# The high and low parts of the activations start where the weights' tiles do, modulo 512 bytes

## The chip, the cores and the metric

The kernel runs on one core of one Trainium2 chip. Its time is the device time of one execution in microseconds (us). Three executions of the kernel before took 716.81, 717.13 and 719.08 us; the median is 717.13 us. The instruments are a hardware profile of one execution (its page and its trace, which can be asked for groups of instructions, waits, the chain of work that ended last, and the instructions in order of time) and, for addresses, the built program.

## The reference, cut to what matters

A two-layer encoder trunk over 512 tokens of width 1024, in float32. The first layer is a Mamba-2 mixer, the second a differential attention:

```python
x = mamba2_layer(x, ...)        # rms_norm, h @ w_in (1024 x 6176), conv, SiLU, chunked scan, gate, @ w_out (2048 x 1024)
kv = rms_norm(x, kv_norm_g) @ w_kv                  # 1024 x 2048, shared keys and values
qg = rms_norm(x, norm_g) @ w_in                     # 1024 x 2048, queries and gate
weights = probs[:, :, 0] - lam * probs[:, :, 1]     # two softmax maps per head, 8 heads
x = x + (out * silu(gate)) @ w_out                  # 1024 x 1024
return rms_norm(x, final_norm_g)
```

Nearly all the arithmetic is in the five large products with a weight matrix. The rest (scan, scores, softmax) is small beside them.

## The kernel before, in words

**Split products.** Each large product runs on TensorE in the type fp32r. To keep float32 accuracy, both factors are split into a high part (rounded to fp32r) and a low part (what is left), and `mm3` (line 243) issues three matmuls: high by high, high by low, low by high. A weight segment arrives by DMA in a tile `raw`; ScalarE writes its high part `whi` (times a gain), VectorE the low part `wlo` (`load`, lines 125 to 179). Two buffers of each rotate. The activations have their own pairs of tiles:

- `hh, hl` (tiles `a_hi`, `a_lo` for the first layer; `b_hi`, `b_lo` for the second, in the same place): the normalised input, 8 blocks of 128 features by 512 tokens (`new_h`, line 342);
- `yh, yl`: the mixer's gated output, per group of 256 features (line 653); the input `xt` shares the buffers of `yl`;
- `oh, ol`: the attention's gated output, per head (line 884).

**What a matmul reads.** TensorE holds one operand of 128 columns in its array (a weight load, LDWEIGHTS, reads it) and streams the other one, 512 columns mostly, past it. While one matmul streams, the load for the next one runs. Both read SBUF. Which tile is loaded and which is streamed differs by product:

| product | PSUM tile | loaded | streamed, columns | matmuls |
|---|---|---|---|---|
| x, B, C of layer 1 | `pg` | `whi`/`wlo` | `a_hi`/`a_lo`, 512 | 768 |
| z of layer 1 | `pz` | `a_hi`/`a_lo` | `whi`/`wlo`, 512 | 384 |
| out projection, layer 1 | `po` | `yh`/`yl` | `whi`/`wlo`, 512 | 384 |
| keys, queries, gate | `pk`, `pq`, `pt` | `whi`/`wlo` | `b_hi`/`b_lo`, 512 | 576 |
| values | `pv` | `b_hi`/`b_lo` | `whi`/`wlo`, 256 | 384 |
| out projection, layer 2 | `pb`, `pc` | `oh`/`ol` | `whi`/`wlo`, 512 | 192 |

The names `po` and `pt` are also used for small float32 matmuls: attention values and states of the scan (`po`), transposed weights of the attention (`pt`). The segment of the out projection that comes last in layer 1 (`("o", 3, 1)`) keeps its split weights in the two buffers of `dec` instead (line 136), 48 of the `po` matmuls.

**Order.** A timeline scheduler of the framework orders the first layer; a dense stream of the large products (`stream_a`) is mixed there with the scan's small matmuls (`ssd`). The second layer's order is written out (`ORDER_B`, `beside`), with the attention of one head beside the dense stream.

**Addresses.** Pools of tiles lie one behind the other in a partition: `const`, `res`, `wp` (`raw`, `whi`, `wlo`), `small`, then the pools of the stage, among them `bp2` (`yl`, `zs`, `xc`, `yh`). A tile starts at a multiple of 32 bytes. `scales` (line 312) takes its tile `r_col`, 16 bytes in a place of 32, from `res`. Every slice that TensorE reads of the tiles above starts a multiple of 512 bytes (128 columns) into its tile, so that all slices of a tile have the tile's own address modulo 512.

Of the kernel before, what the change touches and what calls it, by code (L numbers as in the profile page):

```python
# [9 lines left out]
F32 = mybir.dt.float32  # L10
# [7 lines left out]
P = 128  # L18
S = 512
D = 1024  # L20
NT = S // P
# [42 lines left out]
def trunk(ctx, tc, x, x_t, par, w_dt, w_in, w_out, w_kvqg, w_bo, d_skip, lam_qk, fin_g, out):  # L64
# [4 lines left out]
    const = ctx.enter_context(tc.tile_pool(name="const", bufs=1))  # L69
    res = ctx.enter_context(tc.tile_pool(name="res", bufs=1))  # L70
# [15 lines left out]
    def long_bank(name):  # L86
        return psum.tile([P, 512], F32, tag="long", name=name)
# [163 lines left out]
    def rsqrt(v, n, tag, bufs=2):  # L251


        y = small.tile([P, n], F32, tag=f"{tag}_y", name=f"{tag}_y", bufs=bufs)
        c = small.tile([P, n], F32, tag=f"{tag}_c", name=f"{tag}_c", bufs=bufs)
        iy = small.tile([P, n], I32, tag=f"{tag}_i", name=f"{tag}_i", bufs=bufs)

        def vyy():
            if n == 1:
                V.scalar_tensor_tensor(out=c, in0=y, scalar=v, in1=y, op0=ALU.mult, op1=ALU.mult)  # L260
            else:
                V.tensor_tensor(out=c, in0=y, in1=v, op=ALU.mult)
                V.tensor_tensor(out=c, in0=c, in1=y, op=ALU.mult)

        V.tensor_scalar(out=iy, in0=v.bitcast(I32), scalar1=1, scalar2=None, op0=ALU.logical_shift_right)
        V.tensor_scalar(out=y.bitcast(I32), in0=iy, scalar1=-1.0, scalar2=float(0x5F3759DF - 2 ** 31), op0=ALU.mult, op1=ALU.add)
        vyy()
        V.scalar_tensor_tensor(out=c, in0=c, scalar=-10.0 / 3.0, in1=c, op0=ALU.add, op1=ALU.mult)
        V.scalar_tensor_tensor(out=y, in0=c, scalar=5.0, in1=y, op0=ALU.add, op1=ALU.mult)
        vyy()  # L270
        root_end[0] = V.scalar_tensor_tensor(out=y, in0=c, scalar=-64.0 / 3.0, in1=y, op0=ALU.add, op1=ALU.mult)
        return y
# [39 lines left out]
    def scales(tag, ss):  # L312

        V.tensor_scalar(out=ss, in0=ss, scalar1=ROOT2 / D, scalar2=ROOT2 * EPS, op0=ALU.mult, op1=ALU.add)
        col = res.tile([P, NT], F32, tag="r_col", name=f"{tag}r_col")
        V.tensor_copy(col, rsqrt(ss, NT, "y"))
        w = small.tile([P, NT + 1, P], F32, tag="wide", name=f"{tag}diag", bufs=2)
        GP.memset(w[:, NT], 1.0)
        for t in range(NT):
            GP.tensor_tensor(out=w[:, t], in0=ident, in1=col[:, t:t + 1].to_broadcast([P, P]), op=ALU.mult)  # L320
        ps = long_bank(f"{tag}ps_r")
        T.on = True
        T.matmul(ps, lhsT=w[:, NT], rhs=w[:, 0:NT].rearrange("p t n -> p (t n)"), start=True, stop=True)
        T.on = False
        row = res.tile([P, S], F32, tag="r_row", name=f"{tag}r_row")
        A.copy(row, ps)
        return col, row
# [28 lines left out]
    bctx = ExitStack()  # L356
    bp = bctx.enter_context(tc.tile_pool(name="bp", bufs=1))
    bp2 = bctx.enter_context(tc.tile_pool(name="bp2", bufs=2))

    zt = {}  # L360
    yT = {}
# [42 lines left out]
    for t in range(NT):  # L404
        squares(ss, t)
    r_col, r_row = scales("a", ss)
    V.tensor_scalar(out=sg1, in0=prm[:, C_SG:C_SG + 1], scalar1=0.5 * (1.0 - LAM0), scalar2=None, op0=ALU.mult)
    dtw_raw = sm.tile([P, KD, H], F32, name="dtw_raw")
# [548 lines left out]
    def half(t, n):  # L957
        hs = slice(n * 512, (n + 1) * 512)
        return x_tok[:, t, hs], fg[:, hs], ot[t][:, hs], out[t * P:(t + 1) * P, hs]
# [123 lines left out]
    y, f, o, dst = half(3, 0)  # L1083
# [8 lines left out]
    y, f, o, dst = half(3, 1)  # L1092
# [68 lines left out]
```

## Time and profile before

| | |
|---|---|
| median of three executions | 717.13 us (716.81 to 719.08) |
| the profiled execution: span from its first to its last instruction | 715.2 us |
| TensorE matmuls | 706.5 us busy, 4030 instructions |
| TensorE weight loads | 590.5 us busy |
| VectorE, ScalarE, GpSimd | 521.3, 430.4, 113.5 us busy |
| granted TensorE clock, mean | 0.998 |

How to read it: the matmuls' ends are modelled, and each overlaps the next, so busy TensorE is not TensorE at its peak. What a matmul costs in a stream is its step, the time from its start to the start of the next. The chain of waits lists pieces such as "PE pg L55 x79" with a start and a length: the length over the count is the mean step in that piece. Line 55 is the wrapper through which all instructions of TensorE, VectorE and ScalarE go, so groups are told apart by tiles.

### The profile page before, as it was taken

The page shows a single profiled execution, that of the slowest core. Times are in us where ns is not written, and L with a number is a line of the kernel's source. Part 1 is how long each engine was busy: PE and PEld are TensorE (multiplying, and loading weights), DVE is VectorE, ACT ScalarE, POOL GpSimd, SP SyncE. Part 2 cuts the span into 40 slices and gives each one's busy share as a digit, 9 for nine tenths or more (in the row PEclk, how much of TensorE's full clock was granted, in tenths as well). Part 3 has the DMA queues.
Part 4 walks back from the last instruction along what each step waited for, and adds up shares of the span by engine and source line. Part 5 has one row for each costly group of instructions (what it writes and reads, how often), then busy time and mean ns, then how long its engine had stood idle before and what let it go on. Part 6 is the DMA issues. An engine that isn't in the chain of part 4 may idle for free.

```text
span 715.2 us, 10916 instructions
## 1 busy us (share of the span) xinstructions
PE 706.5 (99%) x4030; PEld 590.5 (83%) x4030; DVE 521.3 (73%) x1197; ACT 430.4 (60%) x955; POOL 113.5 (16%) x158
## 2 busy tenths in 40 slices
PE   9999999999999999999999999999999999999996
PEld 7787888888888888888888879888988898889885
DVE  5579964889579569558996857557667857785886
ACT  6839672664744636537535357667667766765556
POOL 0108411403306025041110101000000000000002
PEclk9999999999999999999999999999999999999999
DMA  8643323233133331331122310421311131122003
GB/s 297 246 177 122 119 62 122 111 119 118 60 118 118 116 120 61 113 123 60 60 81 98 118 59 12 156 77 62 115 60 60 60 119 59 60 80 98 30 0 118
DMA packets 13493, 70.88 MB, mean 99 GB/s; under 512 B 1792, under 2 KB 3328, under 8 KB 6016
## 3 DMA queue, kind: packets, MB, share of 16 engines
q1 hardware_dynamic: 13008, 69.90, 27.3%
q8 instruction: 32, 0.52, 0.3%
q10 hardware_dynamic: 432, 0.28, 0.1%
q14 instruction: 21, 0.17, 0.1%
HBM read 68.02 MB, written 2.16 MB: 98 GB/s over the span
## 4 chain that ended last, share of the span: by engine, by line
PE 90%; ACT 4%; DMA 3%; DVE 2%; issue 1%; SPq 0%; ACTq 0%; DVEq 0%
PE pg L55 21%; PE po L55 17%; PE pz L55 9%; PE pt L55 8%; PE pv L55 6%; PE pq L55 6%; PE pk L55 6%; PE pb L55 3%; PE pc L55 3%; DMA raw<-in_w_in 3%; PE sc L55 3%; PE pyd L55 2%; ACT whi L55 1%; PE pxt L55 1%; PE psA L55 1%; PE pyt L55 1%
## 5 line engine op out<-in xcount | busy, mean ns | idle before, releaser
L55 DVE SCALAR_TENSOR_TENSOR wlo<-raw,prm,whi 128x512 fp32r<-128x512 f32 (+1 forms) x256 | 151.6, 640 | 56.6 <-ACT whi L55 56.2
L55 ACT ACTIVATE whi<-raw,prm 128x512 fp32r<-128x512 f32 (+1 forms) x256 | 136.8, 606 | 65.5 <-issue 13.5
L55 PE MATMUL pg<-a_hi,whi 128*128 128x512 f32 x256 | 103.4, 404 | 0.0
L55 PE MATMUL pg<-a_lo,whi 128*128 128x512 f32 x256 | 102.5, 400 | 0.0
L55 PE MATMUL pg<-a_hi,wlo 128*128 128x512 f32 x256 | 101.3, 401 | 0.0
L55 DVE SCALAR_TENSOR_TENSOR xc<-pg,prc,xc 128x511 f32<-128x511 f32 (+2 forms) x96 | 69.9, 740 | 7.5 <-ACT xc L55 7.1
L55 PEld LDWEIGHTS pg<-a_hi,whi 128*128 128x128 f32 x256 | 48.1, 188 | 11.1 <-issue 0.2
L55 PEld LDWEIGHTS pg<-a_hi,wlo 128*128 128x128 f32 x256 | 48.1, 188 | 11.1
L55 PEld LDWEIGHTS pg<-a_lo,whi 128*128 128x128 f32 x256 | 48.1, 188 | 10.9
L55 PE MATMUL po<-whi,yh 128*128 128x512 f32 x128 | 51.2, 400 | 0.4 <-ACT yh L55 0.4
L55 PE MATMUL po<-wlo,yh 128*128 128x512 f32 x128 | 51.3, 401 | 0.0
L55 PE MATMUL po<-whi,yl 128*128 128x512 f32 x128 | 50.6, 399 | 0.0
L55 PE MATMUL pz<-wlo,a_hi 128*128 128x512 f32 x128 | 50.1, 400 | 0.0
L55 PE MATMUL pz<-whi,a_hi 128*128 128x512 f32 x128 | 49.9, 404 | 0.0
L55 PE MATMUL pz<-whi,a_lo 128*128 128x512 f32 x128 | 49.4, 395 | 0.0
L966 POOL TENSOR_TENSOR ot<-x_tok,fg 128x512 f32<-128x512 f32 x4 | 5.0, 1287 | 248.0 <-DVE x_tok L55 248.0
L55 ACT ACTIVATE s<-s,mx 128x128 f32<-128x128 f32 (+3 forms) x64 | 35.5, 556 | 9.6 <-DVE mx L55 9.1
L593 POOL TENSOR_TENSOR xe<-xdt,tok 128x256 f32<-128x256 f32 x24 | 14.0, 613 | 164.9 <-DVE xdt L55 164.9
L55 ACT ACTIVATE xc<-pg,prc 128x512 f32<-128x512 f32 x32 | 24.8, 775 | 25.0 <-DVE pg L55 19.8
L55 DVE CUSTOM_DVE_ANT_0 s<-sc,bias 128x128 f32<-128x128 f32 (+3 forms) x64 | 29.4, 488 | 12.1 <-PE sc L55 11.7
L55 PE MATMUL pv<-whi,b_hi 128*128 128x256 f32 x128 | 36.6, 286 | 0.0
L55 PE MATMUL pv<-wlo,b_hi 128*128 128x256 f32 x128 | 35.7, 279 | 0.0
(238 smaller groups left out, 1680.5 us busy)
## 6 DMA issues: line engine op xcount, KB each, us to landing
raw<-in_w_in SPq DMA_DIRECT2D x22, 1024.0 KB, 4.8
raw<-in_w_kvqg SPq DMA_DIRECT2D x16, 1024.0 KB, 4.8
dec<-acs_d SPq DMA_DIRECT2D x8, 1024.0 KB, 4.9
raw<-in_w_out SPq DMA_DIRECT2D x8, 1024.0 KB, 4.7
raw<-in_w_bo SPq DMA_DIRECT2D x4, 1024.0 KB, 4.7
x_tok<-in_x SPq DMA_DIRECT2D x4, 512.0 KB, 9.1
out<-ot SPq DMA_DIRECT2D x6, 256.0 KB, 2.4
raw<-in_w_in SPq DMA_DIRECT2D x4, 256.0 KB, 4.5
```

The source lines that it names most:

```text
L55: i = op(*args, **kw)
L593: GP.tensor_tensor(out=xe[:, c], in0=xdt[:, c], in1=toe_tok[:, c, hs].unsqueeze(2).to_broadcast([P, R, HD]), op=ALU.mult)
L966: GP.tensor_tensor(out=o, in0=y, in1=f, op=ALU.mult)
```

## The change

`r_col` is taken from the pool `const` instead of `res`, and the pool `bp2` begins with a tile of 384 bytes that nothing uses:

```diff
     def scales(tag, ss):
...
-        col = res.tile([P, NT], F32, tag="r_col", name=f"{tag}r_col")
+        col = const.tile([P, NT], F32, tag="r_col", name=f"{tag}r_col")
...
     bp2 = bctx.enter_context(tc.tile_pool(name="bp2", bufs=2))
+
+    bp2.tile([P, 96], F32, name="shift", bufs=1)
```

The first edit moves the tiles between the old and the new place of `r_col` up by 32 bytes, the second moves those of `bp2` up by 384. In the built programs the instructions of all engines are the same ones, in the same order, with the same waits; only addresses differ. Modulo 512 bytes:

| tiles | before | after |
|---|---|---|
| `raw`, `whi`, `wlo` | 128 | 128 |
| `a_hi`, `a_lo`, `b_hi`, `b_lo` | 96 | 128 |
| `x_tok` | 96 | 128 |
| `yh`, `yl`, `xt` | 256 | 128 |
| `zs`, `xc` (gate and conv output of layer 1) | 256 | 128 |
| `oh`, `ol`, and the keys and queries of the attention | 128 | 128 |
| `dec` (two buffers; split weights of the segment `("o", 3, 1)`) | 192, 224 | 192, 224 |
| `xdt`, `xe`, `bt`, `hst`, `tmp`, `dx` of the scan | 256 | 256 |
| `ident` | 448 | 448 |

No other tile of any size moves but `dsk` and `tok` (by 32).

## The prediction

> **What bounds the kernel now.** I read the page's busy times first, then busy time by stage, then the chain of waits, then single starts of matmuls.
>
> ```profile
> PE   706.5 (99%) x4030; PEld 590.5 (83%) x4030; DVE 521.3 (73%) x1197; ACT 430.4 (60%) x955; POOL 113.5 (16%) x158
> ...
> PE 90%; ACT 4%; DMA 3%; DVE 2%; issue 1%; SPq 0%; ACTq 0%; DVEq 0%
> ```
>
> The chain that ended last is TensorE's for 90% of the span. By stage:
>
> ```profile
> 0.00:25.60 25.60, 24.13 (x103) 20.04 (x104) 12.96 (x30) 16.38 (x29) 1.06 (x8) 1.00 0.91 331
> ...
> 70.00:345.00 275.00, 275.00 (x1595) 225.85 (x1594) 202.13 (x366) 153.38 (x272) 75.94 (x101) 1.00 0.28 100
> 345.00:430.00 85.00, 84.65 (x503) 69.52 (x502) 66.21 (x136) 39.08 (x85) 10.76 (x16) 1.00 0.24 87
> 430.00:700.00 270.00, 269.95 (x1543) 233.77 (x1542) 194.00 (x567) 179.99 (x498) 5.90 (x9) 1.00 0.20 69
> 700.00:715.20 15.20, 8.89 (x43) 6.76 (x41) 9.73 (x37) 9.46 (x27) 1.91 (x2) 0.93 0.39 139
> ```
>
> The columns are the stretch, its length, then busy us of matmuls, weight loads, VectorE, ScalarE and GpSimd, and the granted clock. From 70 to 700 us TensorE is never seen idle for more than 0.4 us in all, at full clock. Only the first 25.6 us (DMA busy 0.91) and the last 15 wait for others. VectorE is busy 202 of 275 us in the long stage: it has 27% in hand. So the time is set by the step of TensorE's matmuls, and a nanosecond off each step counts. The change adds and removes no instruction; all that it can do is to alter durations and steps.
>
> The step of a 512-column matmul, from the chain of waits (start, length, what):
>
> ```profile
> 86.55 15.63 PE pz L55 x67
> 128.38 18.44 PE pg L55 x79
> 224.11 18.66 PE po L55 x80
> 363.14 18.05 PE po L55 x78
> 398.21 14.50 PE po L55 x62
> 416.52 11.59 PE po L55 x50
> 445.71 11.20 PE pk L55 x48
> ```
>
> 15.63/67 = 233.3 ns for `pz`, 233.4 for `pg`, 233.3 for `pk`; for `po` (18.66+18.05+14.50)/220 = 232.8. The out projection of the second layer, in the same view:
>
> ```profile
> 623.24 2.04 PE pb L55 x9
> ...
> 626.21 2.09 PE pb L55 x9
> ...
> 628.51 4.12 PE pb L55 x18
> ...
> 634.01 2.04 PE pb L55 x9
> ...
> 654.82 2.09 PE pq L55 x9
> ...
> 658.52 2.80 PE pt L55 x12
> ...
> 665.81 4.11 PE pb L55 x18
> ...
> 673.29 2.75 PE pb L55 x12
> ...
> 677.41 2.07 PE pb L55 x9
> ```
>
> The seven pieces of `pb` make 19.22 us for 84 steps: 228.8 ns. Between them stand `pt` with 2.80/12 = 233.3 and `pq` with 2.09/9 = 232.2, so it is not the stage that is quicker. `pb` has the shape of `po` and `pz`: activations loaded, 512 columns of weights streamed, three matmuls per block. What differs is the address: modulo 512, `pb` streams from 128 while it loads from 128; `po` streams from 128 and loads from 256; `pz` 128 and 96; `pg`, `pk`, `pq`, `pt` 96 and 128. The last `po` piece, with weights in `dec`, loads from 256 and streams from 192 or 224: 231.8 on the mean of 50. Its single starts split it into 229.3 (30 steps) where `whi` at 192 streams and 235.9 (16 steps) where `wlo` at 224 does, as here (start and length of each):
>
> ```profile
> 418.92 0.40 PE L55 MATMUL po<-wlo,yh 128*128 128x512 f32 x1
> 419.16 0.39 PE L55 MATMUL po<-whi,yl 128*128 128x512 f32 x1
> ```
>
> Over the 2,094 undisturbed steps of the trace, the difference of the two addresses modulo 512 explains 19% of the variance of the step, modulo 64 only 10%, and modulo 8,192 no more than modulo 512. The two starts lie close, which is how one read can disturb the other:
>
> ```profile
> 100.15 0.39 PE L55 MATMUL pz<-wlo,a_hi 128*128 128x512 f32 x1
> 100.38 0.40 PE L55 MATMUL pz<-whi,a_lo 128*128 128x512 f32 x1
> ```
>
> ```profile
> 100.16 0.19 PEld L55 LDWEIGHTS pz<-whi,a_lo 128*128 128x128 f32 x1
> ```
>
> A matmul starts at 100.15 and the load for the next one at 100.16.
>
> **The change part by part.**
>
> `r_col` to the other pool, first effect: `a_hi`, `a_lo`, `b_hi`, `b_lo` go from 96 to 128, so that `pg`, `pz`, `pk`, `pq`, `pt` get the pair of addresses that `pb` has.
>
> ```profile
> L55 PE MATMUL pg<-a_hi,whi 128*128 128x512 f32 x256 | 103.4, 404 | 0.0
> L55 PE MATMUL po<-whi,yh 128*128 128x512 f32 x128 | 51.2, 400 | 0.4 <-ACT yh L55 0.4
> L55 PE MATMUL pz<-whi,a_hi 128*128 128x512 f32 x128 | 49.9, 404 | 0.0
> L55 PE MATMUL pq<-b_hi,whi 128*128 128x512 f32 x64 | 26.1, 408 | 0.0
> ```
>
> Three such groups each: 768 `pg`, 384 `pz`, 3 x 192 of keys, queries and gate, 1,728 in all. A step gains only where the next load is one of the same product; where a transpose or a scan matmul follows, I count nothing. That leaves 1,633. Each goes from 233.3 to 228.8: 1,633 x 4.5 ns = 7.35 us. The 36 steps or so before 25.6 us lie beside the DMAs that set the pace there: -0.16.
>
> `shift`, first effect: `yh` and `yl` from 256 to 128, so 336 `po` matmuls (the 384 less the 48 from `dec`) get the pair too; 320 of them have one of their own behind them: 320 x (232.8 - 228.8) = 1.28 us. The 48 from `dec` go from differences of 448 and 480 to 64 and 96, which no row shows. Their steps lie between 226 and 237 ns now, so the bound is 48 x 6 = 0.3 us either way; I take 0.
>
> Values (`pv`), 256 columns: 96 against 128 becomes equal as well.
>
> ```profile
> 637.08 3.50 PE pv L55 x30
> ```
>
> ```profile
> L55 PEld LDWEIGHTS pg<-a_hi,whi 128*128 128x128 f32 x256 | 48.1, 188 | 11.1 <-issue 0.2
> L55 PEld LDWEIGHTS pv<-wlo,b_hi 128*128 128x128 f32 x128 | 24.1, 188 | 0.2
> ```
>
> Their step is 116.7 ns, and the weight loads stand idle for only 0.2 us before 128 of them, against 11.1 before 256 of `pg`: loads follow each other without a pause and set the step. I take 0; a gain in proportion (1.9% of 384 x 116.7 ns) would be 0.9 us, and a loss by as much is the other end.
>
> Small float32 matmuls: `xc` moves under the transposes and under the states' product (256 against 256 becomes 256 against 128).
>
> ```profile
> 416.30 0.22 PE pyt L55 x2
> ```
>
> ```profile
> 643.55 0.44 PE pt L55 x4
> ```
>
> The transposes step at 110 ns with the loaded tile at 256 (`pyt`) and at 128 (`pt`) alike: 0. The 48 matmuls of the states could at worst lose what `po` lost, 48 x 4.5 = 0.2 us.
>
> Other engines: do their durations depend on the address?
>
> ```profile
> L55 DVE TENSOR_TENSOR yl<-pyt,yh 128x512 fp32r<-128x512 f32 x14 | 9.0, 685 | 4.8 <-ACT yh L55 4.8
> L55 DVE TENSOR_TENSOR b_lo<-btp,b_hi 128x512 fp32r<-128x512 f32 x8 | 5.1, 684 | 2.9 <-ACT b_hi L55 2.9
> L55 DVE TENSOR_TENSOR ol<-og,oh 128x512 fp32r<-128x512 f32 x7 | 4.8, 690 | 2.5 <-ACT oh L55 2.5
> ```
>
> The same subtraction takes 685 ns at 256, 684 at 96 and 690 at 128, and VectorE's spare 27% hides 1% more: 0. Without that cover, 6 ns on each of its 1,197 instructions would be 7 us.
>
> What TensorE gives back: it arrives earlier at loads whose operand ScalarE or VectorE has yet to write. The page shows 0.4 us of such idling in the body, but steps of 242 ns and more, which the modelled ends hide, add up to some 12 us over the step of 233, by the single starts. Between two of these a quicker stream only waits longer. I take 15% of the gain, 1.3 us; the bounds are none and half.
>
> Sum: 7.35 + 1.28 - 0.16 - 1.3 = 7.2 us. The profiled execution's span, 715.2, becomes 708.0. The median stands 1.9 us above that span, in what lies around it; that stays: **709.9, say 710.0 us**. The bounds of the new step are the quickest `pb` piece (2.04/9 = 226.7) and the slowest (2.09/9 = 232.2). The first, with nothing given back: 1,633 x 6.6 + 320 x 6.1 = 12.7 us, 704.4. The second: 1,633 x 1.1 + 320 x 0.6 = 2.0, 715.1. Cases near the middle are likelier, since 84 steps average 228.8: 706.5 to 713 for the forecast alone.
>
> **The rivals.**
>
> *No change: the address is not the cause.* The streamed and the loaded operand may not disturb each other at all, and `pb` may be quicker for what its tiles are: `oh` and `ol` were written long before, say, while `yh` and `b_hi` are fresh. For it: the steps of `pb` vary within the group, 226.7 to 232.2 by piece, at one address. Against it: `pt` in the same 50 us is at 233.3 in step, and in the `dec` piece the step is 229.3 or 235.9 by the streamed tile's address, with the same fresh `yh` and `yl`. Time: 717.1, within 2.15. The Trainium skill's "TensorE: Matmul & The Clock Gate", Part 2, step 1 (LDWEIGHTS), holds this view: TensorE has two independent read ports, and loading the next weights takes no read bandwidth from the running matmul. By that rule the sum is 0 and the time 717.1; the rows of `pb` and `pt` above, 228.8 against 233.3, speak against it.
>
> *Quicker steps, given back.* The scan of layer 1 and the attention are chains through ScalarE and VectorE. If TensorE is at their pace already, half or more of 8.5 us turns into waits: 717.1 - 3.5 = 713.6. For it: the 12 us of long steps. Against it: 0.4 us of idling seen, 27% in hand.
>
> *Slower: what counts is not equality.* Two pairs with the same difference of 480 step differently, 235.9 (224 against 256) and 233.2 (96 against 128), so the difference alone does not fix the step. If in the first layer's stream, with tiles of rows 2 KB long, equal addresses meet in the same place again and again, the step goes to the slowest pair seen: 1,953 x (235.9 - 233.2) = 5.3 us, 722.4. It decides once `pg` steps above 234.3 (717.13 + 2.15). Against it: `pb` streams rows of 2 KB from the same tiles, and steps at 228.8.
>
> **How the numbers follow.** Forecast 0.78, no change 0.11, given back 0.06, slower 0.05. A measurement of this kernel can tell about 0.3%, 2.15 us. Faster (below 714.98) holds the forecast and nearly all of the third case: 0.83; the same 0.12; slower 0.05. The range of 8 in 10 reaches from 706.0, inside the bound of the quickest step, up to 714.5, over the third case.
>
> **What would show it.** In the chain of waits of the changed kernel, pieces of `pg`, `pz` and `pk` of 48 and more should stand at 227 to 230 ns each, as `pb` does, and `po` likewise, with `pb` and `pc` unchanged; `pv` at 117; the same subtractions at 684 to 690 ns; idle TensorE in the body below 2 us. Steps of 233 in `pg` would make the account of the addresses wrong; steps of 229 with a time above 714 would make the 15% wrong.

## The result

The changed kernel takes 709.23 us (median of four executions, 708.80 to 709.89) against 716.97 us (the kernel before, now with a fourth execution of 716.68): a ratio of 0.9889, 95% interval 0.9875 to 0.9904. That is 7.7 us less. The forecast was 710.0, in a range of 706.0 to 714.5. The profiled execution took 709.26 us with a span of 707.5 us; before, the span was 715.2.

The page of the changed kernel, busy time and chain:

```profile
PE 697.5 (99%) x4030; PEld 590.8 (84%) x4030; DVE 519.5 (73%) x1197; ACT 430.1 (61%) x955; POOL 111.7 (16%) x158
...
PE 88%; ACT 4%; DVE 3%; DMA 3%; issue 1%; SPq 0%; ACTq 0%; DVEq 0%
```

Only TensorE's matmuls lost a good deal of busy time, 9.0 us. The weight loads (590.5 before), ScalarE, VectorE and GpSimd are within 2 us of what they were. The chain of waits shows the same pieces as before, with the same counts (start, length, what):

```profile
68.11 5.95 PE pg L55 x26
...
86.41 15.22 PE pz L55 x67
...
127.43 17.96 PE pg L55 x79
...
221.26 18.19 PE po L55 x80
...
357.67 17.73 PE po L55 x78
...
392.23 14.28 PE po L55 x62
410.34 11.57 PE po L55 x50
433.93 5.75 PE pv L55 x48
439.68 10.91 PE pk L55 x48
...
620.84 4.09 PE pb L55 x18
```

15.22/67 = 227.2 ns for `pz` (233.3 before), 17.96/79 = 227.3 for `pg` (233.4), 10.91/48 = 227.3 for `pk` (233.3), (18.19+17.73+14.28)/220 = 228.2 for `po` (232.8). The out projection of layer 2, whose addresses were equal already, stays: 4.09/18 = 227.2 here, 228.9 in the piece that answers to it before, and over all undisturbed steps 228.7 against 229.0 for `pb` and 229.7 against 229.1 for `pc`. The values step at 5.75/48 = 119.8 ns. Before, the same piece was shorter:

```profile
440.05 5.67 PE pv L55 x48
```

That is 118.1 ns. The piece of `pg` at 68.11 began at 68.05 before: in the first 68 us nothing was won, and all of the 7.7 us lies behind.

### The profile page after: what moved, and what is told of

Same layout as the page of the kernel before. It is cut to its first block, busy times and chain, and to the rows that moved or that the text cites. A ratio compares the mean times of both kernels' runs of the same rounds, so it can differ in the third digit from the quotient of the medians.

```text
span 707.5 us, 10916 instructions
## 1 busy us (share of the span) xinstructions
PE 697.5 (99%) x4030; PEld 590.8 (84%) x4030; DVE 519.5 (73%) x1197; ACT 430.1 (61%) x955; POOL 111.7 (16%) x158
## 4 chain that ended last, share of the span: by engine, by line
PE 88%; ACT 4%; DVE 3%; DMA 3%; issue 1%; SPq 0%; ACTq 0%; DVEq 0%
PE pg L55 20%; PE po L55 16%; PE pz L55 9%; PE pt L55 7%; PE pv L55 6%; PE pq L55 6%; PE pk L55 6%; PE pb L55 3%; DMA raw<-in_w_in 3%; PE sc L55 3%; PE pyd L55 2%; PE pc L55 2%; ACT whi L55 1%; PE pxt L55 1%; PE psA L55 1%; PE pyt L55 1%
## 5 line engine op out<-in xcount | busy, mean ns | idle before, releaser
L55 PE MATMUL pv<-whi,b_lo 128*128 128x256 f32 x128 | 36.2, 283 | 0.0
```

The costliest lines, as they stand in the source:

```text
L55: i = op(*args, **kw)
```

## The experiments

All kernels below issue the same instructions in the same order with the same waits as the two compared kernels; only addresses differ, so that nothing of the computation is changed or left out. Edits are shown against the changed kernel. "Step" is start to start of two matmuls of one product, with 512 columns unless said otherwise; steps of 242 ns and more (with 256 columns, of 130) are left out as stalls. "Difference" is the address of the streamed tile less that of the tile loaded for the next matmul, modulo 512 bytes.

### Each edit alone

`r_col` in the other pool, without the 384 bytes:

```diff
-    bp2.tile([P, 96], F32, name="shift", bufs=1)
```

> r_col moved alone: a_hi, a_lo, b_hi, b_lo lie at 128 like the weights, yh and yl stay at 256. If the step of a matmul follows the pair of addresses (the tile it streams, the tile loaded for the next one), pg and pz step at 227 to 228 ns and pk, pq, pt at 228 to 229, po stays at 232.8 (before: 233.3, 233.3, 233.0, 232.8), pv at 119.5 (before 117.0), and the time falls by 7.7 less what po gives, 1.5: about 6.2 us, 710.8. If the two edits only work together (all tiles in one place), neither alone gives more than 2 us: 715 or more.

Measured: 711.48 us, ratio 0.9926 (0.9909 to 0.9942), 5.7 us less than the 717.21 us of before beside it. Chain of waits:

```profile
86.40 15.21 PE pz L55 x67
127.44 17.95 PE pg L55 x79
...
221.37 18.66 PE po L55 x80
...
435.52 5.75 PE pv L55 x48
441.27 10.91 PE pk L55 x48
```

`pz`, `pg`, `pk` have the quick step (227.0, 227.2, 227.3), `po` has the old one (18.66/80 = 233.3, the very length of before).

The 384 bytes alone:

```diff
-        col = const.tile([P, NT], F32, tag="r_col", name=f"{tag}r_col")
+        col = res.tile([P, NT], F32, tag="r_col", name=f"{tag}r_col")
```

> The 384 bytes alone: yh and yl at 128 like the weights, a_hi, a_lo, b_hi, b_lo stay at 96. By the pair of addresses po steps at 227.8 and pg, pz, pk stay at 233, pv at 117.0: 320 steps by 4.9 ns are 1.6 us, 715.4. The two edits together should then add up to the 7.7 us of the change. If xc and zs (which move as well) mattered to VectorE or ScalarE, the conv's and gate's instructions would differ from 739 and 550 ns.

Measured: 715.63 us, ratio 0.9979 (0.9970 to 0.9989), 1.6 us less. Chain of waits:

```profile
86.41 15.64 PE pz L55 x67
128.26 18.44 PE pg L55 x79
...
223.88 18.18 PE po L55 x80
...
438.43 5.67 PE pv L55 x48
444.10 11.20 PE pk L55 x48
```

The reverse picture: only `po` is quick (18.18/80 = 227.3). 5.7 and 1.6 make 7.3 us, against 7.7 together: the two edits work each on its own products. VectorE's instructions on the moved `xc` keep their 739 to 742 ns; those on `zs` take 535 instead of 550 ns, 0.5 us in all on an engine with time in hand.

### Equality or alignment

96 is an odd multiple of 32, 128 and 256 are not, so that the change could have helped by alignment. One more tile of 32 bytes ahead of `x_tok` puts activations and weights at 160 together:

```diff
+    res.tile([P, 8], F32, name="pad_a")
     x_tok = res.tile([P, NT, D], F32, name="x_tok")
```

> The change with 32 bytes more ahead of x_tok: activations and weights lie at 160 all together, equal modulo 512 but no longer a multiple of 64 or 128. If equality of the two counts, all steps stay as after the change (227 to 229 ns) and the time is 709.2. If what counts is each tile's own address (96 and 224 are odd multiples of 32, 128 and 256 are not), 160 is as bad as 96: pg and pz step at 233 or more and the time goes back to 717.

Measured: 709.46 us, ratio 0.9896 (0.9881 to 0.9910). Chain of waits:

```profile
86.56 15.22 PE pz L55 x67
127.59 17.96 PE pg L55 x79
...
221.47 18.19 PE po L55 x80
```

To 10 ns the lengths of the changed kernel. Equality of the two addresses counts; their own place does not, as far as 128 and 160 show.

### Which load disturbs which stream

As `r_col` alone, with the low parts 32 bytes further than the high parts:

```diff
-    hh, hl = new_h("a")
+    hi_ = res.tile([P, KD, S], F32R, tag="hT_hi", name="a_hi")
+    res.tile([P, 8], F32, name="pad_a")
+    hh, hl = hi_, res.tile([P, KD, S], F32R, tag="hT_lo", name="a_lo")
+    res.tile([P, 120], F32, name="pad_b")
```

> As col_only, but the low parts a_lo and b_lo lie 32 bytes further, at 160, while a_hi, b_hi and the weights are at 128. If a step depends on the streamed tile and on the load for the NEXT matmul, pg is slow (231 to 235) only where a_lo streams (a third of its steps), and pz only in the step before the one that loads a_lo, that of wlo,a_hi where whi,a_lo follows. If it depends on the streamed tile and the matmul's OWN loaded tile, pz is slow in the step of whi,a_lo itself. If the streamed tile's own address alone counts, pg is slow where a_lo streams and pz nowhere. Time: a third of the 6.2 us of r_col is lost, 712.9.

Measured: 716.32 us in one execution; the expected 712.9 was 3.4 us too low. In order of time, z of layer 1 (start, length of each):

```profile
96.93 0.40 PE L55 MATMUL pz<-whi,a_hi 128*128 128x512 f32 x1
97.16 0.40 PE L55 MATMUL pz<-wlo,a_hi 128*128 128x512 f32 x1
97.40 0.39 PE L55 MATMUL pz<-whi,a_lo 128*128 128x512 f32 x1
97.63 0.40 PE L55 MATMUL pz<-whi,a_hi 128*128 128x512 f32 x1
97.86 0.40 PE L55 MATMUL pz<-wlo,a_hi 128*128 128x512 f32 x1
98.10 0.39 PE L55 MATMUL pz<-whi,a_lo 128*128 128x512 f32 x1
```

The long step, 0.24 us, is each time that of `wlo,a_hi`, the matmul during which `a_lo` is loaded for the next one; the matmul that uses `a_lo` steps at 0.23. Over 116 steps the first is 237.5 ns on the mean; over 109 the second is 229.3. In `pg` the step while `a_lo` streams is the long one (234.3 over 231). So the pair is the streamed tile and the load for the next matmul; neither the matmul's own load nor the streamed tile's own address fits both products.

What the expectation missed is that the steps with equal addresses suffer too. In `pz` the third one, `whi,a_hi`, has 232.0 ns, in `pg` the other two 231.6 and 229.9, where the kernel with all tiles equal has 227 to 228. A single unequal pair in three costs nearly as much as three: `pz` averages 15.62/67 = 233.1. How one step reaches into the next is not shown.

```profile
86.61 15.62 PE pz L55 x67
128.45 18.31 PE pg L55 x79
```

### How far apart, and the period

The activations of the projections lie X bytes beyond the weights, with a tile of X bytes ahead of them and one of 512 - X behind; `yh`, `yl` move by `shift`. Here X = 64 (128, 192 and 256 alike, with `shift` of 192, 224 and 64 bytes):

```diff
+    res.tile([P, 16], F32, name="pad_a")
     hh, hl = new_h("a")
+    res.tile([P, 112], F32, name="pad_b")
...
-    bp2.tile([P, 96], F32, name="shift", bufs=1)
+    bp2.tile([P, 32], F32, name="shift", bufs=1)
```

> Activations of the projections 64 bytes beyond the weights (192 against 128), yh and yl at 384. Differences (streamed less loaded, modulo 512): pg, pk, pq, pt 64; pz and pv 448; po 256. If the difference alone sets the step, pg and pk step at 231 as the dec segment does at 64 after the change, pz at 229.3 as it does at 448 before it; po at 256 is new: 232 to 233 if any odd difference costs what 384 costs, 227 to 228 if half the period is as good as none. Time about 713.

> As the last, 128 bytes apart: pg, pk, pq, pt 128; pz and pv 384; po 192. By the difference alone pz steps at 232.7 (po before the change has 384); pg at 128 is new: 232 to 233 if the cost is about the same for all far differences, near 227 if only the nearest (32, 64, 96) disturb. Time 716 to 717 by the first, 713 by the second.

> 192 bytes apart: pg, pk, pq, pt 192; pz and pv 320; po 160. None has been seen. 232 to 234 and a time of 716 to 717 if the cost is about the same for all far differences; 227 to 229 and 709 to 711 if only near ones disturb.

> 256 bytes apart, half the period: pg, pk, pq, pt, pz and pv all 256; po 320. 232 to 234 and 716 to 717 by the same account; if the period were 256 and not 512, this would be as good as equal, 227 to 228 and 710 to 711. pv (256 columns, 119.5 where equal, 117.0 at 32): near 117 if any difference spares it.

Measured, one execution each: 711.21, 717.15, 717.50 and 710.63 us; the reading rests on the steps, which many matmuls share, and not on these single times. Chain of waits of the two outer ones, X = 64 first:

```profile
86.44 15.63 PE pz L55 x67
128.11 18.08 PE pg L55 x79
...
222.92 18.19 PE po L55 x80
...
436.45 5.46 PE pv L55 x48
441.92 10.99 PE pk L55 x48
```

X = 256:

```profile
87.20 15.22 PE pz L55 x67
128.25 17.95 PE pg L55 x79
...
435.27 5.76 PE pv L55 x48
441.02 10.91 PE pk L55 x48
```

At X = 256 `pz` and `pg` have the lengths of the changed kernel, and `po` in the X = 64 run (difference 256) too: the period is 256 bytes, not 512. Mean steps in ns by difference modulo 256, from all runs in which a whole product has one difference (`po` without the `dec` segment):

| difference modulo 256 | `pg` | `pz` | `po` | `pv`, 256 columns |
|---|---|---|---|---|
| 0 | 227.7 | 227.3 | 227.8 | 119.5 |
| 32 | | 233.3 | | 117.0 |
| 64 | 229.2 | 229.7 | 229.4 | 117.5 |
| 128 | 232.6 | 232.4 | 232.6 | 118.6 |
| 160 | | | 234.2 | |
| 192 | 233.3 | 233.3 | 233.3 | 115.4 |
| 224 | 233.2 | | | |

Whichever of the two is the activation, the step is the same to 0.5 ns. It is not symmetric: 64 is nearly as good as 0, 192 is as bad as 224. The expected 229.3 for `pz` at 448 (192 modulo 256) was wrong, 233.3: it came from the `dec` segment, in which this pair alternates with one at 480, and after the finding above such a mixture is no measure of one pair. For the same reason the 235.9 and 233.2 ns that the prediction sets against each other at one difference of 480 do not show that a difference has two steps. At X = 192 neither expected case holds for all products: `pg` steps at 233.3, `pz`, 64 apart modulo 256, at 229.7. At X = 256 `pv` steps as at equality (119.6) and not near 117. For the 256-column matmuls equality is the worst of the differences tried, and 192 the best.

### A version that takes both

Layer 2 only: `b_hi` and `b_lo` 64 bytes further, so that `pk`, `pq`, `pt` have a difference of 64 and `pv` one of 192; layer 1 as after the change, modulo 256.

```diff
-        return [res.tile([P, KD, S], F32R, tag=f"hT_{i}", name=f"{tag}_{i}") for i in ("hi", "lo")]
+        at = 16 if tag == "b" else 0
+        return [res.tile([P, KD * S + 64], F32R, tag=f"hT_{i}", name=f"{tag}_{i}")[:, at:at + KD * S].rearrange("p (k s) -> p k s", k=KD) for i in ("hi", "lo")]
...
-    bp2.tile([P, 96], F32, name="shift", bufs=1)
+    bp2.tile([P, 32], F32, name="shift", bufs=1)
```

> The change, but the second layer's b_hi and b_lo lie 64 bytes beyond the weights (192 or 448 against 128) while the first layer's a_hi, a_lo stay equal to them modulo 256, and yh, yl lie at 384. From the runs with 64 and 256 bytes: pk, pq, pt step at 229.5 instead of 228.6 (some 520 steps, +0.4 us), pv at 115.4 instead of 119.5 (384 steps, -1.6 us), po and pg as after the change. Time 708.0 against the change's 709.2. If pv's steps lie on cover that hides them (the projections of the second layer wait for ScalarE and VectorE), or the 0.4 us is all that reaches the end, 709.2 to 709.6.

> The changed kernel beside it on the same chip, for the comparison: 709.2 us, ratio to before 0.989.

Measured side by side: 708.66 us (708.31 to 710.13), ratio 0.9886 (0.9864 to 0.9907), and for the changed kernel 709.47 us (708.99 to 709.83), ratio 0.9890 (0.9874 to 0.9905). The 0.8 us between the medians have the expected sign and two thirds of the size, but the times alone do not separate the two. The chain of waits shows where they are:

```profile
410.04 11.57 PE po L55 x50
433.46 5.46 PE pv L55 x48
438.92 10.99 PE pk L55 x48
```

`pv` steps at 5.46/48 = 113.8 instead of 119.8 in that piece, `pk` at 229.0 instead of 227.3. From the `po` piece at 410 us to the end of the span it is 706.4 - 410.0 = 296.4 us, against 707.5 - 410.3 = 297.2 after the change. The second trace of the changed kernel, with a span of 707.8 us, is 0.3 us later at that piece (410.68) and also has 297.2 from there on; behind 71 us the starts of all matmuls in these two traces stay 0.32 to 0.36 us apart. So about 0.8 us come from the second layer; 0.3 of the 1.1 us between the spans 707.5 and 706.4 lie ahead of 410 us, where the two kernels have the same steps.

## Why the prediction was right, and where its terms were off

**What bounds the kernel**: right, from 68 us on. A nanosecond off the step came out at the end, as the two single edits show (5.7 and 1.6 us from two disjoint sets of products).

**The pair of addresses as the cause**: right. `pb` in the profile of before was a fair sample of what the other products would do. The alternative by which `pb` was quick for other reasons than its address falls with each edit alone: with `yh` written as late as before, `po` went to 18.18/80 = 227.3 ns. The Trainium skill's "TensorE: Matmul & The Clock Gate", Part 2, step 1, by which loading the next weights takes no read bandwidth from the running matmul, stands for that alternative. The steps of `pz` here differ from it: 227.2 and 233.3 ns with nothing changed but the address of what is loaded. The slower case falls with `pg` at 227.3.

**The terms.** The step fell further than the 4.5 ns taken: by 5.7 in `pg` (233.3 to 227.6, undisturbed steps), 6.1 in `pz`, 4.4 in the projections of layer 2, 4.9 in `po`. Over the steps of each in the trace of before: 726 x 5.7 + 372 x 6.1 + 535 x 4.4 + 320 x 4.9 = 10.3 us, where the prediction had 7.35 + 1.28 = 8.6. The 84 steps of `pb` were too slow a sample: they mix steps of up to 229 ns (64% of the undisturbed ones) with 231 to 236, and after the change the first kind makes 85% of `pg` and 91% of `pz`. The prediction's bound of 6.6 ns a step covers it.

`pv` was taken at 0, with 0.9 us of loss as the other end. That end came: 117.0 to 119.5 ns over 384 steps, 1.0 us. Weight loads after the change:

```profile
L55 PEld LDWEIGHTS pg<-a_hi,wlo 128*128 128x128 f32 x256 | 48.1, 188 | 9.8
...
L55 PEld LDWEIGHTS pv<-wlo,b_hi 128*128 128x128 f32 x128 | 24.5, 191 | 0.2
```

They take 191 ns each in `pv` against 188 before, and still follow each other with no idle time. That the loads set the step fits this, but is not shown: at steps of 115.4, 117.0 and 118.6 ns the loads alike take 187 to 189.

What TensorE gives back: 10.3 - 1.0 - 7.7 = 1.6 us, where 1.3 + 0.16 = 1.5 was taken, the 0.16 for the head. The amount was fair, the reason was not. It was put down to long steps all over the body. Instead most of it lies in one stretch. The span of the chain from 25.6 to 68 us is the same before and after, piece by piece; here after the change:

```profile
26.43 1.93 ACT whi L55 x3
...
46.16 2.74 DVE wlo L55 x4
...
60.88 1.93 ACT dec L55
...
64.48 0.64 ACT xc L55
65.17 0.66 PE pxt L55 x4
```

ScalarE and VectorE make the time steps, the decays and the first convolution there, and TensorE waits at the first transposes of the scan for the convolution. This wait was 0.3 us before:

```profile
PE pxt L55 <- ACT xc L55: 0.3, 1, 0.3
```

After the change it is 1.4:

```profile
PE pxt L55 <- ACT xc L55: 1.4, 1, 1.4
```

The matmuls are busy for most of that stretch, before and after (length, then busy us of the matmuls), so that it looked like TensorE's:

```profile
25.60:70.00 44.40, 43.88 (x253) 34.61 (x252) 36.29 (x64) 32.15 (x47) 17.94 (x24) 1.00 0.40 149
```

```profile
25.60:68.10 42.50, 40.63 (x241) 32.24 (x240) 33.62 (x60) 29.94 (x46) 15.70 (x20) 1.00 0.41 152
```

Its idle time grew from 0.5 to 1.9 us. Start by start, the same matmul comes 1.0 us earlier after the change at 63.7 us, and 0.1 later at 65.4, behind the wait for the convolution. Of some 2,180 steps 232 lie before 68 us; at 5.7 ns they are 1.3 us that could not come out. The step that failed is the prediction's reading that only the first 25.6 us wait for others. Its count for that head is wrong too: the trace has 86 such steps there, not 36. Behind 68 us the measured sizes, the loss of `pv` included, make 8.0 us, and 7.7 came out. Two of the prediction's signs failed with these terms: `pv` is not at 117, and TensorE idles 2.3 us between 25.6 and 692 us, where less than 2 was expected.

That 7.2 us was forecast and 7.7 came is in part luck: the step was taken 1.7 us too small and `pv` 1.0 us too favourable, and the two misses work against each other.

One illustration of the prediction is misread. The two matmuls that it shows for the `dec` segment, at 418.92 and 419.16, lie ahead of it: its 48 begin at 419.62, and these two step at 232 and 231 ns. The figures beside them, 229.3 over 30 steps and 235.9 over 16, are those of the segment.

**Costs taken as nothing**: right. The subtractions take 683 ns (`yl`, at 128 now), 683 (`b_lo`) and 689 (`ol`, not moved), as before to 2 ns; the 45 undisturbed steps of the `dec` segment went from 231.6 to 232.3 on the mean; the states' product and the transposes kept their steps to 1 ns.

```profile
L55 DVE TENSOR_TENSOR yl<-pyt,yh 128x512 fp32r<-128x512 f32 x14 | 9.0, 683 | 4.3 <-ACT yh L55 4.3
L55 DVE TENSOR_TENSOR b_lo<-btp,b_hi 128x512 fp32r<-128x512 f32 x8 | 5.1, 683 | 3.0 <-ACT b_hi L55 3.0
```

## What to carry to other kernels

When TensorE is the bound, compute its step (length over count of long pieces in the chain) for each product and compare products of the same shape: a difference of 2% is worth a question, and the addresses of the two operands are one of the answers. Steps of one shape in an undisturbed part of the same trace priced the change to a fifth here (8.6 us taken, 10.3 found). Look also at which stages are truly paced by the engine: a stretch can show TensorE busy throughout and still have a chain that goes through other engines. Addresses move with any new tile in an earlier pool, so that a change of 1% in an unrelated edit may be this.

## What the runs showed that was not expected

- The period is 256 bytes of the partition: a difference of 256 gives 227 to 228 ns as 0 does, 128 gives 232.4 to 232.6.
- The cost is not symmetric: a streamed tile 64 bytes beyond the loaded one costs 2 ns, one 64 bytes behind (192) costs 6.
- One unequal pair in three slows the two equal ones as well (229 to 232 ns instead of 227 to 228).
- In fp32r matmuls of 256 columns, where the loads follow each other with no idle time, equal addresses are the slowest (119.5 ns) and a difference of 192 the quickest (115.4).

How the reads get in each other's way is not shown by these runs. They show which two reads it is, the period, and that it happens at the full granted clock (0.997 to 0.999 in all of them).
